# Two steps of the second compression placed later in the list of work

## The chip, the cores and the metric

The kernel runs on one core of a Trainium2 chip. The metric is the device time of one execution in microseconds, as the median of several runs. The engines are TensorE (PE in the profile, its weight loads PEld), VectorE (DVE), ScalarE (ACT), GpSimd (POOL) and SyncE (SP, which here only issues transfers).

## The reference, cut to what matters

One layer of a transformer on 512 tokens of width 1024: a mixer, a cross attention over 256 memory tokens and a gated feed-forward, each between norms. The mixer holds sparse attention beside an mLSTM. The change touches two parts of the mixer:

```python
def compress_blocks(kv, pos, w1, w2):            # once for k, once for v
    ...
    blocks = jnp.concatenate([c[:, :, :-1], c[:, :, 1:]], axis=3) + pos
    hid = jax.nn.silu(blocks.reshape(B, H, -1, CMP_BLOCK * DH) @ w1)   # (.., 2048) @ (2048, 256)
    return hid @ w2
...
    y_ml = jax.nn.sigmoid(mo) * hm               # mo: 512 columns of h @ w_in, the output gates
```

The compressed v is needed only by the compressed branch of the attention. `hm` is the mLSTM's output, of four heads.

## The kernel before

Every product of float32 matrices is made of three products in a shorter format: ScalarE writes a rounded copy of the weights (`hi`), VectorE or GpSimd subtracts it from the original (`lo`), and TensorE runs `lo*hi`, `hi*lo`, `hi*hi` (`split`, L166 and L167; `mm3`, L286 to L288). A tile of 128 output columns over 512 tokens (`dense_tiles`, L293 ff.) is thus one ScalarE copy and one subtraction of 128x1024 and 24 matmuls 512 columns wide into one PSUM bank.

After the first stage (norm of x, values, gates) comes a stage of mixed work, whose list is the string `order` in `PLAN`:

- `c0`, `c1`: projections of the mLSTM's q and k with their convolution (`ev_conv`, on VectorE); `kc`: projections that feed the two compressions (`ev_kcvc`); `m0`, `m2`: the four tiles of the output gates `mo`; `ks`: keys of the attention; `q0`: queries. Each has two tiles, and each mention of the name runs one of them. Their weights arrive in two buffers `raw`, filled by SP's queue; `hi` and `lo` (`whi`, `wlo`) take one each of **four** buffers `W`.
- `Sn`: the mLSTM's scores of head n (`mlstm_scores`): ScalarE and VectorE make `qm`, `kmA`, `kmB`; a row comes from DRAM into `rb` by a transfer that ScalarE's queue issues (L746); GpSimd adds a mask to it (`dg`, L748); ScalarE takes exponentials (L763); TensorE makes four blocks of scores, each in one of three PSUM banks `sc`; VectorE multiplies (L765). `On`: that head's output (`mlstm_out`: matmuls `bk_mn`, transposes `bk_mt`).
- `Lk`, `Lv`: loads of the compressions' weights; `Ck`, `Cv`: the compressions (`comp`), in four steps each. A step takes two of eight weight pieces (`w1s`). A piece is split in one buffer that holds `hi` and `lo` side by side, and is the moving side of two matmuls 512 wide into the bank `hb`, which is one of the three `sc` banks from the first step to the last. All eight pieces of `Cv` use the four `W` buffers (`"w1tv": "WWWWWWWW"`), and `"w1v": "pvpvvppv"` gives the engine of each subtraction: of pieces 0 to 7, numbers 0, 2, 5 and 6 on GpSimd and the rest on VectorE. Behind the eighth piece `comp_out` reads the bank.

The order on each engine is not the list's alone: a scheduler simulates the program at compile time and gives a free engine the first instruction in the list that its simulation holds ready. `S` and `O` are moved up in the list by 100 places (`mprio`). Buffers are handed out in the order so found. On the chip each engine then runs its queue in order.

The loop that reads the list is at the end of the stage's definitions:

```python
    for op in PLAN["order"].split():
        if op in whole:
            if op not in begun:
                begun[op] = whole[op]()
            run(begun[op], 1)
```

Of the kernel before, what the change touches and what calls it, by code (L numbers as in the profile page):

```python
# [47 lines left out]
def hybrid_layer(ctx, tc, a, out):  # L48
# [19 lines left out]


# [2 lines left out]

# [1 line left out]

# [1355 lines left out]
def build(inputs):  # L1430
    import numpy as np
    import concourse.bacc as bacc

    nc = bacc.Bacc("TRN2", target_bir_lowering=False, num_devices=1, dynamic_dma_scratch_size=1024)
    arrays, args = {}, {}
    for name in _INS + ["consts"]:
        v = np.ascontiguousarray(inputs[name] if name != "consts" else host_constants())
        arrays[f"in_{name}_dram"] = v
        args[name] = nc.dram_tensor(f"in_{name}_dram", v.shape, mybir.dt.from_np(v.dtype), kind="ExternalInput").ap()
    o = nc.dram_tensor("out_0_dram", (1, S, D), F32, kind="ExternalOutput").ap()  # L1440
    with tile.TileContext(nc, schedule_with_timeline_sim=True) as tc:
        hybrid_layer(tc, args, o)
    return nc, arrays
# [8 lines left out]
```

## Time and profile before

| | us |
|---|---|
| median of 3 runs | 838.19 |
| lowest, highest | 837.92, 840.44 |
| profiled execution, its own time | 842.27 |
| its span, as the profile shows it | 840.5 |

The span runs from the first to the last instruction of the profiled execution; 1.77 us of its own time lie around it. Times in the rows below are microseconds from the span's start. The stretch around the change lies between 100 and 145 us; the attention begins at some 165 us, and the rest follows to 840.5 us.

### The profile page before, as it was taken

The page shows a single profiled execution, that of the slowest core. Times are in us where ns is not written, and L with a number is a line of the kernel's source. Part 1 is how long each engine was busy: PE and PEld are TensorE (multiplying, and loading weights), DVE is VectorE, ACT ScalarE, POOL GpSimd, SP SyncE. Part 2 cuts the span into 40 slices and gives each one's busy share as a digit, 9 for nine tenths or more (in the row PEclk, how much of TensorE's full clock was granted, in tenths as well). Part 3 has the DMA queues.
Part 4 walks back from the last instruction along what each step waited for, and adds up shares of the span by engine and source line. Part 5 has one row for each costly group of instructions (what it writes and reads, how often), then busy time and mean ns, then how long its engine had stood idle before and what let it go on. Part 6 is the DMA issues. An engine that isn't in the chain of part 4 may idle for free.

```text
span 840.5 us, 12639 instructions
## 1 busy us (share of the span) xinstructions
PE 818.5 (97%) x4838; PEld 706.2 (84%) x4838; DVE 535.3 (64%) x936; ACT 424.8 (51%) x840; POOL 290.8 (35%) x218
## 2 busy tenths in 40 slices
PE   8999989989999999999999999999999999999997
PEld 6877858876689878778888899999999999888885
DVE  5766684897889735743553779877888885124323
ACT  5535566768768643633543465444444444334311
POOL 1015331455537343501420101444444444323320
PEclk9999989999999999999999999999999999999999
DMA  8238312221102431243323034333333323222102
GB/s 249 75 106 259 110 52 81 82 70 63 63 14 89 150 102 51 100 150 101 101 101 100 10 117 152 119 109 106 114 103 103 102 101 101 101 101 100 51 26 76
DMA packets 67763, 83.18 MB, mean 99 GB/s; under 512 B 4368, under 2 KB 53873, under 8 KB 67702
## 3 DMA queue, kind: packets, MB, share of 16 engines
q1 hardware_dynamic: 64574, 77.97, 28.8%
q10 hardware_dynamic: 3128, 4.40, 1.7%
q8 instruction: 38, 0.62, 0.3%
q14 instruction: 23, 0.19, 0.1%
HBM read 80.24 MB, written 2.12 MB: 98 GB/s over the span
## 4 chain that ended last, share of the span: by engine, by line
PE 88%; DVE 7%; ACT 2%; issue 2%; DMA 1%; POOL 0%; SPq 0%; DVEq 0%; ACTq 0%; POOLq 0%
PE bk_dT L286 6%; PE bk_dT L287 6%; PE bk_dT L288 6%; PE bk_X L1300 5%; PE bk_X L1301 5%; PE bk_X L1302 5%; PE bk_ff L287 5%; PE bk_ff L288 5%; PE bk_ff L286 5%; PE bk_pv L1026 3%; PE bk_dN L287 3%; PE bk_dN L286 3%; PE bk_dN L288 3%; PE bk_Z L1300 2%; PE bk_Z L1301 2%; PE bk_Z L1302 2%
## 5 line engine op out<-in xcount | busy, mean ns | idle before, releaser
L166 ACT ACTIVATE whi<-raw 128x1024 fp32r<-128x1024 f32 (+1 forms) x80 | 76.8, 967 | 72.0 <-PE bk_dT L286 35.3
L167 DVE TENSOR_TENSOR wlo<-raw,whi 128x1024 fp32r<-128x1024 f32 x43 | 56.7, 1322 | 85.9 <-PE bk_ff L287 43.0
L167 POOL TENSOR_TENSOR wlo<-raw,whi 128x1024 fp32r<-128x1024 f32 x21 | 50.3, 2396 | 121.4 <-ACT whi L166 119.5
L166 ACT ACTIVATE wh<-raw 128x1024 fp32r<-128x1024 f32 x64 | 67.2, 1057 | 49.3 <-PE bk_X L1300 17.7
L167 POOL TENSOR_TENSOR wl<-raw,wh 128x1024 fp32r<-128x1024 f32 x19 | 55.4, 2917 | 97.3 <-ACT wh L166 69.9
L286 PE MATMUL bk_dT<-hTh,wlo 128*128 128x512 f32 x192 | 77.6, 404 | 1.2 <-DVE wlo L167 0.9
L287 PE MATMUL bk_dT<-hTl,whi 128*128 128x512 f32 x192 | 76.9, 400 | 0.0
L288 PE MATMUL bk_dT<-hTh,whi 128*128 128x512 f32 x192 | 76.4, 398 | 0.0
L167 DVE TENSOR_TENSOR wl<-raw,wh 128x1024 fp32r<-128x1024 f32 x45 | 65.7, 1465 | 9.3 <-ACT wh L166 9.3
L1301 PE MATMUL bk_X<-A,wh 128*128 128x256 f32 x192 | 54.5, 284 | 1.0 <-DVE A L167 1.0
L167 POOL TENSOR_TENSOR gs<-gf,gs 128x512 fp32r<-128x512 f32 x22 | 32.4, 1477 | 65.9 <-ACT gs L166 65.9
L1300 PE MATMUL bk_X<-A,wl 128*128 128x256 f32 x192 | 54.4, 283 | 0.4 <-ACT A L166 0.4
L1302 PE MATMUL bk_X<-A,wh 128*128 128x256 f32 x192 | 54.3, 283 | 0.0
L287 PE MATMUL bk_ff<-wlo,gs 128*128 128x512 f32 x128 | 49.8, 389 | 0.0
L288 PE MATMUL bk_ff<-whi,gs 128*128 128x512 f32 x128 | 49.6, 389 | 0.0
L1300 PE MATMUL bk_X<-AS,wl 128*128 128x256 f32 x160 | 45.6, 285 | 2.4 <-ACT u L1355 2.3
L286 PE MATMUL bk_ff<-whi,gs 128*128 128x512 f32 x128 | 47.4, 389 | 0.0
L996 POOL TENSOR_SCALAR s<-s,acf 128x128 f32<-128x128 f32 (+3 forms) x32 | 36.3, 1146 | 26.7 <-PE bk_tr L1011 15.9
L286 PEld LDWEIGHTS bk_dT<-hTh,wlo 128*128 128x128 f32 x192 | 36.6, 191 | 10.4 <-DVE wlo L167 2.1
L1302 PE MATMUL bk_X<-AS,wh 128*128 128x256 f32 x160 | 44.9, 281 | 0.0
L1300 PE MATMUL bk_Z<-AS,wl 128*128 128x256 f32 x160 | 44.9, 280 | 0.0
L1301 PE MATMUL bk_X<-AS,wh 128*128 128x256 f32 x160 | 44.8, 280 | 0.0
(376 smaller groups left out, 2527.9 us busy)
## 6 DMA issues: line engine op xcount, KB each, us to landing
raw<-in_w_gate_up_dram SPq DMA_DIRECT2D x22, 1024.0 KB, 5.5
raw<-in_w_down_dram SPq DMA_DIRECT2D x11, 1024.0 KB, 4.9
raw<-in_w_xkv_dram SPq DMA_DIRECT2D x8, 1024.0 KB, 5.3
raw<-in_w_in_dram SPq DMA_DIRECT2D x7, 1024.0 KB, 5.2
raw<-in_w_out_dram SPq DMA_DIRECT2D x4, 1024.0 KB, 5.0
raw<-in_w_xq_dram SPq DMA_DIRECT2D x4, 1024.0 KB, 5.2
raw<-in_w_xo_dram SPq DMA_DIRECT2D x4, 1024.0 KB, 5.0
raw<-in_w_in_dram SPq DMA_DIRECT2D x6, 512.0 KB, 4.8
```

What stands on the lines that cost most here:

```text
L166: first = nc.scalar.activation(hi, src, AF.Copy)
L167: second = (eng or nc.vector).tensor_tensor(lo, src, hi.bitcast(F32), op=OP.subtract)
L286: nc.tensor.matmul(o, lhsT=wl, rhs=xh, start=start, stop=False)
L287: nc.tensor.matmul(o, lhsT=wh, rhs=xl, start=False, stop=False)
L288: return nc.tensor.matmul(o, lhsT=wh, rhs=xh, start=False, stop=stop).ins
L996: ENG[on].tensor_scalar(s[:, 0:n], s[:, 0:n], c, None, op0=OP.mult)
L1026: nc.tensor.matmul(o, lhsT=v, rhs=pTs[br][q][:, j], start=(br, j, q) == mms[0], stop=(br, j, q) == mms[-1])
L1300: nc.tensor.matmul(o, lhsT=wl[:, k, c], rhs=A.hi(n, k), start=st, stop=False, skip_group_check=True)
L1301: nc.tensor.matmul(o, lhsT=wh[:, k, c], rhs=A.lo(n, k), start=False, stop=False, skip_group_check=True)
L1302: nc.tensor.matmul(o, lhsT=wh[:, k, c], rhs=A.hi(n, k), start=False, stop=stop and k == 3, skip_group_check=True)
```

## The change

The list is rearranged in one place. The first and second step of `Cv` stay; the third comes behind the first tile of `m2`, and the fourth behind `S2`, ahead of the second tile of `m2`:

```diff
         "order": "c0 Lk c0 Lv kc m0 m0 Ck Ck Ck Ck c1 kc S0 O0 c1 "
-                 "S1 Cv Cv Cv Cv m2 S2 m2 O2 ks O1 ks q0 S3 q0 O3",
+                 "S1 Cv Cv m2 Cv S2 Cv m2 O2 ks O1 ks q0 S3 q0 O3",
```

No instruction, transfer or buffer is added or removed by name; their order, and what the scheduler makes of it, is all that differs.

## Rows read from the trace of the kernel before

**Rows 1.** The page, busy time of each engine and share of the span.

```profile
PE 818.5 (97%) x4838; PEld 706.2 (84%) x4838; DVE 535.3 (64%) x936; ACT 424.8 (51%) x840; POOL 290.8 (35%) x218
```

**Rows 2.** Busy time in stretches: bounds, length, each engine (instructions), granted clock, DMA, GB/s.

```profile
100.00:110.00 10.00, 10.00 (x54) 8.48 (x53) 9.52 (x24) 9.13 (x25) 3.27 (x4) 1.00 0.53 139
110.00:120.00 10.00, 7.56 (x29) 4.27 (x27) 9.62 (x20) 7.34 (x16) 5.48 (x4) 0.90 0.00 1
120.00:130.00 10.00, 9.22 (x34) 7.47 (x35) 5.23 (x11) 3.88 (x11) 2.64 (x3) 0.76 0.42 133
```

**Rows 3.** TensorE in order of time: start, length, line, tiles, [idle before, releaser].

```profile
110.80 1.18 PE L879 MATMUL bk_hb<-w1s,Xb 128*128 128x512 f32 x4
111.81 1.05 PE L776 MATMUL bk_mn<-mvx,sT 128*128 128x129 f32 x8
113.11 1.58 PE L879 MATMUL bk_hb<-w1s,Xb 128*128 128x512 f32 x4 [0.24 <-POOL w1s L167]
116.36 2.03 PE L879 MATMUL bk_hb<-w1s,Xb 128*128 128x512 f32 x6 [1.67 <-DVE w1s L167]
118.66 1.22 PE L879 MATMUL bk_hb<-w1s,Xb 128*128 128x512 f32 x2 [0.27 <-DVE w1s L167]
120.78 0.80 PE L286 MATMUL bk_dT<-hTh,wlo 128*128 128x512 f32 x1 [0.90 <-DVE wlo L167]
...
128.04 0.39 PE L288 MATMUL bk_dT<-hTh,whi 128*128 128x512 f32 x1
```

**Rows 4.** TensorE in one microsecond: bounds, length, busy, granted clock, DMA, GB/s.

```profile
118.00:119.00 1.00, 0.73 (x3) 0.50 0.00 0
```

**Rows 5.** The chain that ended last, pieces in order of time: start, length, what.

```profile
85.23 0.92 PE bk_hb L879 x4
...
122.85 0.43 PE bk_dT L287
```

**Rows 6.** ScalarE in order of time.

```profile
112.36 2.20 ACT L166 ACTIVATE w1s<-w 128x512 fp32r<-128x512 f32 x4
...
117.13 1.06 ACT L166 ACTIVATE whi<-raw 128x1024 fp32r<-128x1024 f32 x1 [1.77 <-PE bk_hb L879]
...
122.50 0.33 ACTq L746 DMA_DIRECT2D rb<-rd  x1
...
142.41 1.06 ACT L166 ACTIVATE whi<-raw 128x1024 fp32r<-128x1024 f32 x1 [2.87 <-PE bk_dT L286]
```

**Rows 7.** VectorE in order of time.

```profile
113.23 0.68 DVE L167 TENSOR_TENSOR w1s<-w,w1s 128x512 fp32r<-128x512 f32 x1
...
113.89 0.74 DVE L712 SCALAR_TENSOR_TENSOR zc<-u,chan,zc 128x509 f32<-128x509 f32 x1
114.55 1.75 DVE L167 TENSOR_TENSOR w1s<-w,w1s 128x512 fp32r<-128x512 f32 x1
...
119.51 2.35 DVE L167 TENSOR_TENSOR wlo<-raw,whi 128x1024 fp32r<-128x1024 f32 x2
```

**Rows 8.** GpSimd in order of time.

```profile
114.10 3.35 POOL L167 TENSOR_TENSOR w1s<-w,w1s 128x512 fp32r<-128x512 f32 x2 [1.05 <-ACT w1s L166]
...
128.33 1.28 POOL L748 TENSOR_TENSOR dg<-rb,cc 128x512 f32<-128x512 f32 x1 [4.62 <-DMA rb<-rd]
```

**Rows 9.** Splits of the tile `w1s` from 100 to 120; ns min/median/max, first and last start.

```profile
L166 ACT ACTIVATE w1s<-w x8: 613/620/631, 103.1 to 114.7; 128x512 fp32r<-128x512 f32 x8
L167 POOL TENSOR_TENSOR w1s<-w,w1s x4: 1385/1633/1737, 103.8 to 115.7; 128x512 fp32r<-128x512 f32 x4
L167 DVE TENSOR_TENSOR w1s<-w,w1s x4: 679/689/1755, 106.8 to 117.9; 128x512 fp32r<-128x512 f32 x4
```

**Rows 10.** The same view for `wlo` on VectorE from 40 to 260.

```profile
L167 DVE TENSOR_TENSOR wlo<-raw,whi x9: 1211/1224/1599, 39.8 to 168.5; 128x1024 fp32r<-128x1024 f32 x9
```

**Rows 11.** Issues of SP's queue in order of time.

```profile
121.88 16.45 SPq L300 DMA_DIRECT2D raw<-in_w_in_dram  x2
...
171.15 1.29 SPq L442 DMA_DIRECT2D nB<-fd  x3
```

## The prediction

> **What bounds the kernel now.** I read the page first: TensorE is busy for 97% of the span and no other engine for more than 64% (VectorE) [rows 1]. So the end moves by what TensorE loses or wins back, and a change in the order of work can win only where TensorE stands still or runs slowly. The second view was the table of stretches. It shows such a place in the middle of the second compression: TensorE is fully busy from 100 to 110, busy for 7.56 of 10 us in the next stretch, and from 120 to 130 it is busy again but at a granted clock of 0.76 on average [rows 2]. The engine that is full there is VectorE, with 9.52 and 9.62 of 10 us [rows 2].
>
> The third view, TensorE in order of time, tells what happens. The 16 matmuls of `Cv` begin at 110.80 and the last pair starts at 118.66 and after; between them TensorE waits for a subtraction on GpSimd, for one on VectorE (1.67 us) and for a second one (0.27 us), and then 0.90 us more for the `wlo` of the first tile of `m2` [rows 3]. A busy time in these rows covers pipelined matmuls; the starts are what count. While TensorE worked this thinly its clock fell: at 118 to 119 it is at 0.50 [rows 4], that is the lower of its two levels, 1.2 instead of 2.4 GHz, and a 512 wide matmul takes 0.43 us where four take 0.92 us, 0.23 each, at the upper level [rows 5]. Nine of the 24 matmuls of the first `m2` tile run so, 9 x (0.43 - 0.23) = 1.8 us.
>
> How much is there to win? From 110.80 the work is 16 matmuls of `Cv` at 0.23 (3.7 us), the eight `bk_mn` (1.0 us) and 24 of `m2` at 0.23 (5.5 us): 10.2 us, which would end at 121.0. The 24th starts at 128.04 [rows 3] and ends at 128.27. So 7.3 us are lost here, 0.9% of the time, and that is the ceiling of the gain.
>
> **Why TensorE waits.** The eight pieces share the four buffers `W`. ScalarE copies pieces 3 to 6 in a row from 112.36 as the matmuls of earlier pieces free a buffer, then the first `whi` of `m2` has to wait for the matmuls on `hb` (1.77 us idle) and starts at 117.13 [rows 6]. VectorE has the subtraction of piece 3 until 113.91, steps of c1's convolution (`zc`), piece 4 for 1.75 us, and only at 119.51 the two `wlo` [rows 7]; GpSimd subtracts pieces 5 and 6 from 114.10 to 117.45 [rows 8]. TensorE has 24 matmuls of `m2` to do that depend on nothing of this, whose weights are there, but whose buffers and VectorE's time come behind all of `Cv`.
>
> **The change, step by step.** It adds and removes no instruction. It puts the `hi` and `lo` of the first `m2` tile ahead of pieces 4 to 7. The steps, each from the rows of before:
>
> 1. Up to piece 3 all stays. ScalarE has copied piece 3 by 112.36 + 2.20/4 = 112.9. The buffers of pieces 0 and 1, which went to pieces 4 and 5, now go to `whi` and `wlo`. `whi` takes 1.06 us [rows 6]: 114.0.
> 2. VectorE is done with piece 3 at 113.91; I leave the `zc` step of 0.74 us in front, to 114.6 [rows 7]. `wlo` takes 1.22 us (median) [rows 10]: 115.8. TensorE has by then finished pieces 2 and 3, at about 114.5, and waits 1.3 us.
> 3. The 24 matmuls run from 115.8 for 5.5 us at the upper level, to 121.3. They cover the splits of pieces 4 and 5, for which two buffers are left: 0.62 us on ScalarE each, then at most 1.76 us on VectorE and 1.74 us on GpSimd [rows 9]. If this cover were gone they would cost what they cost now.
> 4. Pieces 4 and 5, four matmuls, 0.92 us: 122.2.
> 5. Pieces 6 and 7 get the buffers that `m2` leaves at 121.3: 0.62 us on ScalarE, 1.39 us for piece 6 on GpSimd [rows 9], ready at 123.3. TensorE waits 1.1 us, then 0.92 us: 124.2. This is the new wait that the change brings; ahead of it on TensorE the scores of `S2` may fill it, which I don't count.
> 6. The second `m2` tile, which before was split together with the first (2.35 us for both `wlo` [rows 7]) and ready at once, takes the buffers of pieces 4 and 5. ScalarE is done with piece 7 at 122.5; `whi` 1.06 and `wlo` 1.22 us: 124.8. TensorE waits 0.6 us.
>
> The second tile thus starts at 124.8 instead of 128.27, a gain of 3.5 us. Of the 7.3 us, 3.8 thus stay: the three waits of steps 2, 5 and 6 (3.0 us) and what pieces 2 and 3 lose up to 114.5 now as before (0.8 us).
>
> **The queues and what comes after.** Neither moved step issues a transfer on SP's queue: `Lv` stays. SP's next read of weights, at 121.88, waits until the second `m2` tile is split, at 121.86 before and 124.8 now; its first user on ScalarE stands at 142.41 [rows 6, 11], so 2.9 us later costs nothing. The last step issues one small transfer on ScalarE's queue (`w2`), whose result is wanted behind `comp_out`. What `comp_out` makes, the compressed v, is wanted only where the attention's units end, so a later end of `Cv` costs nothing by itself; but `hb` keeps one of three `sc` banks while `S2` wants four in turn. From `S2` on nothing is bound to the clock on the wall: even the last loads of the bias tables, issued at 171.15 [rows 11], wait for buffers that TensorE's own `bk_mn` frees. So the 3.5 us should last to the end.
>
> By the profiled execution: 842.27 - 3.5 = 838.8 us. That execution is 4.1 us above the median of the runs, so for the median I take 838.19 - 3.5 = **834.7 us**. The bounds of this case: with every wait gone, 838.19 - 7.3 = 830.9; with the waits of steps 2, 5 and 6 longer by a third (1.0 us in all), 835.7. 0.3% is 2.5 us, about what a measurement of this kernel can tell from no change.
>
> **Rival 1: GpSimd's queue, slower.** `S2` stands now ahead of the last step of `Cv`. Its `dg` waits on GpSimd for the row `rb` from DRAM: the transfer was issued at 122.50 [rows 6] and `dg` ran only at 128.33, after 4.62 us of standing still [rows 8]. If the scheduler's simulation holds `dg` ready before piece 6, the subtraction of piece 6 is queued behind it and starts at 128.33 + 1.28 = 129.6; it is ready at 131.0, the four matmuls end at 131.9, and the second `m2` tile starts 3.6 us later than before and, behind such a gap, at the lower clock (1.8 us): 838.19 + 5.4 = 843.6. It decides from the point where piece 6 is ready later than 128.1. For it: `S2` is ahead in the list and moved up by 100 places. Against it: before, GpSimd got `dg` 11 us after its last piece [rows 8], and piece 6 needs to come only by 123.3. Chance 0.20.
>
> **Rival 2: VectorE slowed beside GpSimd, no change.** The same subtraction of `w1s` takes 0.69 us on VectorE in the median and 1.755 us where GpSimd's pieces 5 and 6 run beside it [rows 7, 8, 9]. If piece 5 on GpSimd falls on the `wlo` of step 2, that takes 1.22 x 1.755/0.689 = 3.1 us, 1.9 us more, and the gain is 1.6 us: 836.6. If the clock falls too in the longer gap, nothing is left: 838.4. I put the change nearer to 1.22 because piece 5 has to wait for a buffer that piece 3 frees at 114.5 and for a copy of 0.62 us, so that most of `wlo` is past by then; the largest of nine `wlo` is 1.599 us [rows 10]. The Trainium skill, page "GPSIMD Engine Reference", section "Key points", says that GpSimd shares its interfaces to SBUF with VectorE and that they contend when VectorE reads two inputs from SBUF, as this subtraction does; the trace agrees, with 1.755 against 0.689 us, and by that rule taken for the whole of `wlo` the time would be 836.6. Chance 0.14.
>
> **Rival 3: the change doesn't do what it says.** The list is not the queue. `S` and `O` move, and the simulation may hand the buffers to pieces 4 to 7 first anyway, as their copies need only ScalarE. Then TensorE's order stays nearly as it is: 838.2. Against it: before, the engines' order around `Cv` and `m2` is the list's. Chance 0.14.
>
> **How the numbers follow.** The forecast has 0.52, the rivals 0.20, 0.14 and 0.14. Faster is the forecast alone, 0.52; within 0.3% are rivals 2 and 3, 0.28; slower is rival 1, 0.20. The predicted time is the forecast's. Its own range is 830.9 to 835.7. For eight in ten the range has to take in the cases without change up to the 2.5 us that count as such, so 830.9 to 840.7; the slower rival stays outside.
>
> **What would show it.** Right: on TensorE four `bk_hb` pairs, then `bk_dT` without a break at some 115 to 121, then `bk_hb` again; `wlo` on VectorE near 114.6 instead of 119.51; a clock that doesn't fall, or for fewer than the nine `m2` matmuls of before; the start of the second `m2` tile near 124.8. The forecast is wrong if a piece of `Cv` stands on GpSimd behind `dg` or another instruction that waits (rival 1), if `wlo` takes around 3 us (rival 2), if `whi` still stands behind piece 7 on ScalarE (rival 3), or if a wait that did not exist opens behind 145 us, which would mean that the order further down was rearranged too.

## The result and the profile after

| | us | runs |
|---|---|---|
| kernel before, median (lowest to highest) | 838.92 (837.92 to 840.44) | 4 |
| changed kernel, median (lowest to highest) | 844.70 (843.31 to 846.22) | 4 |
| ratio, 95% interval | 1.0072 [1.0055, 1.0088] | |
| predicted | 834.7 (830.9 to 840.7), faster | |

The change made the kernel slower by 0.7%. The prediction is 10 us off and on the wrong side. The profiled execution of the changed kernel took 844.43 us of its own time, with a span of 842.6 us.

The table of stretches comes first, with the same columns as [rows 2]; the last two stretches lie far behind the change.

```profile
110.00:120.00 10.00, 8.49 (x39) 6.26 (x38) 9.18 (x20) 5.69 (x14) 3.60 (x3) 1.00 0.00 1
120.00:130.00 10.00, 7.77 (x31) 5.68 (x30) 9.05 (x15) 8.62 (x19) 6.33 (x8) 0.90 0.21 59
...
128.00:129.00 1.00, 1.00 (x4) 0.77 (x3) 1.00 (x3) 1.00 (x2) 0.12 (x1) 0.50 0.44 42
...
150.00:160.00 10.00, 9.13 (x48) 7.23 (x47) 6.74 (x14) 8.81 (x23) 4.64 (x3) 1.00 0.26 73
180.00:200.00 20.00, 15.18 (x75) 11.04 (x73) 17.59 (x58) 13.47 (x39) 14.05 (x11) 0.91 0.17 54
```

From 100 to 110 TensorE is busy throughout, as before. From 110 to 120 TensorE is busier than before, 8.49 against 7.56 us, at full clock; from 120 to 130 it is less busy, 7.77 against 9.22 [rows 2]. The gain is there and is given back within ten microseconds, with a stretch at the lower level of the clock behind it (0.50 at 128 to 129; before it was at 118 [rows 4]). From 150 to 160 TensorE was busy throughout in the trace of before and is now for 9.13 us.

TensorE in order of time shows the local part; these rows answer to [rows 3].

```profile
113.15 1.59 PE L879 MATMUL bk_hb<-w1s,Xb 128*128 128x512 f32 x4 [0.24 <-POOL w1s L167]
115.87 0.50 PE L286 MATMUL bk_dT<-hTh,wlo 128*128 128x512 f32 x1 [1.13 <-DVE wlo L167]
...
121.53 1.10 PE L879 MATMUL bk_hb<-w1s,Xb 128*128 128x512 f32 x4
123.75 0.74 PE L879 MATMUL bk_hb<-w1s,Xb 128*128 128x512 f32 x2
125.72 0.73 PE L879 MATMUL bk_hb<-w1s,Xb 128*128 128x512 f32 x2 [1.23 <-DVE w1s L167]
127.45 0.49 PE L286 MATMUL bk_dT<-hTh,wlo 128*128 128x512 f32 x1 [1.00 <-DVE wlo L167]
```

The first `m2` tile, pieces 4 and 5, piece 6, piece 7 and the second `m2` tile follow each other. The other three engines, in the same view:

```profile
114.60 1.22 DVE L167 TENSOR_TENSOR wlo<-raw,whi 128x1024 fp32r<-128x1024 f32 x1
...
122.84 1.14 DVE L723 TENSOR_SCALAR sg<-sg,chan 128x512 f32<-128x512 f32 x1 [0.33 <-ACT sg L722]
123.90 1.76 DVE L167 TENSOR_TENSOR w1s<-w,w1s 128x512 fp32r<-128x512 f32 x1
125.59 0.68 DVE L795 TENSOR_TENSOR ym<-bk_mt,sg 128x512 f32<-128x512 f32 x1
126.19 1.21 DVE L167 TENSOR_TENSOR wlo<-raw,whi 128x1024 fp32r<-128x1024 f32 x1
...
123.57 0.99 ACT L763 ACTIVATE sT<-rb,ub 128x128 f32<-128x128 f32 x3 [0.23 <-DMA rb<-rd]
124.46 1.04 ACT L166 ACTIVATE whi<-raw 128x1024 fp32r<-128x1024 f32 x1
...
122.41 1.29 POOL L167 TENSOR_TENSOR w1s<-w,w1s 128x512 fp32r<-128x512 f32 x1 [0.81 <-ACT w1s L166]
123.66 1.46 POOL L748 TENSOR_TENSOR dg<-rb,cc 128x512 f32<-128x512 f32 x1
125.17 2.20 POOL L733 MEMSET kB<- 64x512 f32 x4
```

Piece 6 on GpSimd comes ahead of `dg`. Piece 7 on VectorE takes 1.76 us, with `dg` beside it on GpSimd, in place of 0.69 [rows 9]. On ScalarE the `whi` of the second tile stands behind the first exponentials of `S2`.

The next place is 25 us further down. GpSimd, VectorE, TensorE:

```profile
152.46 1.29 POOL L748 TENSOR_TENSOR dg<-rb,cc 128x512 f32<-128x512 f32 x1 [24.33 <-DMA rb<-rd]
153.71 1.03 POOL L236 TENSOR_TENSOR rs_r<-rs_e,mhalf 128x4 f32<-128x4 f32 x1
154.70 2.39 POOL L167 TENSOR_TENSOR wlo<-raw,whi 128x1024 fp32r<-128x1024 f32 x1
...
154.77 3.00 DVE L790 TENSOR_SCALAR hnat<-hnat,rs_r 128x128 f32<-128x128 f32 x4 [2.17 <-POOL rs_r L236]
...
157.32 0.30 PE L791 MATMUL bk_mt<-cc,hnat 128*128 128x128 f32 x1 [0.28 <-DVE hnat L790]
159.48 0.47 PE L286 MATMUL bk_dT<-hTh,wlo 128*128 128x512 f32 x1 [0.59 <-DVE kB L841]
```

In the trace of before, TensorE has no wait of 0.1 us or more from 136 to 165. Here `rs_r`, the factor that scales head 2's output, comes behind `S3`'s `dg`. The four scalings of `hnat` then begin together with GpSimd's residual split of `q0`'s second tile and take 3.00 us, where those of an earlier head take 0.86 us at 121.66. And at the attention's start, VectorE and TensorE:

```profile
179.01 1.14 DVE L447 COPY nB<-nB 128x256 f32<-128x256 f32 x1 [0.63 <-DMA nB<-fd]
180.07 0.41 DVE L683 TENSOR_TENSOR pc<-pc,bk_pc 128x256 f32<-128x256 f32 x1
...
183.14 1.09 DVE L687 TENSOR_TENSOR pc<-pc,mn 128x512 f32<-128x512 f32 x1
...
187.31 0.63 PE L697 MATMUL bk_pcT<-cc,pc 128*128 128x128 f32 x4 [1.68 <-ACT qst L827]
189.52 0.69 PE L791 MATMUL bk_mt<-cc,hnat 128*128 128x128 f32 x2 [1.36 <-DVE hnat L790]
```

The last bias tables are loaded from 175.62 on, 4.5 us later than before [rows 11]. VectorE's copy of one of them (head 6's) now stands in the middle of the chain on `pc`, the compressed branch's probabilities, ahead of the second `bk_pc` addition. In the trace of before it is done by 177.0, ahead of the chain's first addition at 177.39:

```profile
176.54 0.43 DVE L447 COPY nB<-nB 128x256 f32<-128x256 f32 x1
```

From its first addition to its last product (L694) the chain takes 10.8 us here and 9.2 us in the trace of before. The row of `bk_pcT` names ScalarE's `qst`, which ended just before; but in both traces the transposes start 0.15 us behind the end of the last product on `pc`, so it is the chain that they wait for.

**Where the time is lost.** To compare executions at equal work, I went through TensorE's instructions and took from the time that had passed what each kind takes when it runs without a gap at the upper level (0.23 us for 512 columns; from the kernel before). What is left was lost to waits and to the lower clock. The segments have the same amount of work in every kernel; in the trace of before they end at some 111, 140, 165 and 230 us.

| us lost by TensorE | up to `Cv` | `Cv`, `m2` | to the attention | its first units | rest | span |
|---|---|---|---|---|---|---|
| before (the profile of the prediction) | 11.3 | 8.3 | 1.2 | 11.4 | 30.8 | 840.5 |
| before, a second profile (e1) | 10.0 | 6.4 | 1.2 | 11.7 | 31.1 | 837.9 |
| after | 11.3 | 7.7 | 2.6 | 13.1 | 30.4 | 842.6 |

Nothing that the change moves stands ahead of `Cv`, so the first column differs by chance (8.5 to 11.4 us over all profiles here). The clock differs by chance too: before and e1 have the same instructions in the same order, and their 1.9 us in the second column are nearly all of it clock. Against e1, the changed kernel is 4.7 us longer: 1.3 of it ahead of the change, 1.3 in `Cv` and `m2`, 2.8 in the two segments behind, less 0.7 in the rest.

### The profile page after: what moved, and what is told of

Its sections match the earlier page's. It is cut to its first block, busy times and chain, and to the rows that moved or that the text cites. A ratio compares the mean times of both kernels' runs of the same rounds, so it can differ in the third digit from the quotient of the medians.

```text
span 842.6 us, 12635 instructions
## 1 busy us (share of the span) xinstructions
PE 816.8 (97%) x4838; PEld 705.0 (84%) x4838; DVE 533.7 (63%) x936; ACT 424.5 (50%) x840; POOL 290.9 (35%) x218
## 4 chain that ended last, share of the span: by engine, by line
PE 71%; DVE 6%; ACT 2%; issue 1%; POOL 0%; DMA 0%; DVEq 0%; ACTq 0%; POOLq 0%
PE bk_X L1300 5%; PE bk_X L1301 5%; PE bk_X L1302 5%; PE bk_ff L286 5%; PE bk_ff L288 5%; PE bk_ff L287 5%; PE bk_pv L1026 3%; PE bk_dT L286 3%; PE bk_dT L287 3%; PE bk_dT L288 3%; PE bk_dN L287 3%; PE bk_dN L286 3%; PE bk_dN L288 3%; PE bk_Z L1300 2%; PE bk_Z L1301 2%; PE bk_Z L1302 2%
## 5 line engine op out<-in xcount | busy, mean ns | idle before, releaser
L167 POOL TENSOR_TENSOR wlo<-raw,whi 128x1024 fp32r<-128x1024 f32 x21 | 50.5, 2405 | 119.2 <-ACT whi L166 109.7
```

The costliest lines, as they stand in the source:

```text
L167: second = (eng or nc.vector).tensor_tensor(lo, src, hi.bitcast(F32), op=OP.subtract)
```

## The experiments

The theories went in with letters. A: the loss comes from the order further down. B: it comes from new waits beside the change. C: the profile that I started from was an unlucky one. Later D stands for the two places further down, L for the local part and P for the chain on `pc`. Each time is a median of 4 to 12 runs; each ratio is to runs of the kernel before on the same chip, and four chips were used.

| run | median, us | ratio to before, 95% interval |
|---|---|---|
| e1 before, unchanged | 839.10 | 0.9995 [0.9981, 1.0009] |
| e2 `Cv` together, `S2` behind `m2` | 840.05 | 1.0007 [0.9991, 1.0023] |
| e3 step 4 alone moved | 842.40 | 1.0046 [1.0029, 1.0063] |
| e4 after, `dg` behind `rs_r` | 844.77 | 1.0058 [1.0036, 1.0080] |
| e5 after, head 6's copy on ScalarE | 843.23 | 1.0043 [1.0027, 1.0060] |
| e6 after, `q0`'s second split on VectorE | 841.24 | 1.0022 [1.0009, 1.0035] |
| e7 after, both | 839.19 | 0.9996 [0.9984, 1.0009] |
| e8 step 4 behind the second `m2` tile | 843.80 | 1.0048 [1.0030, 1.0065] |
| e9 before, both edits | 840.59 | 1.0021 [1.0000, 1.0042] |
| e10 e8, both edits | 840.78 | 1.0022 [1.0007, 1.0036] |
| e11 e8, head 6's copy on ScalarE, one split at 227 us moved | 842.09 | 1.0033 [1.0014, 1.0051] |
| e12 e7, head 2's `dg` on VectorE | 843.48 | 1.0052 [1.0035, 1.0069] |
| e13 e10, `pc` chain one unit later | 847.42 | 1.0100 [1.0080, 1.0121] |
| e14 e10, `pc` chain two units later | 847.72 | 1.0104 [1.0083, 1.0124] |
| e15 before, `pc` chain one unit later | 842.23 | 1.0042 [1.0025, 1.0059] |

### Before again, and the parts of the order (e1 to e4)

e1 has no edit. 

> The kernel before, unchanged. Theory C (the profiled execution of before was an unlucky one, 842.27 against a median of 838.9, because TensorE's clock stood at half for 6.8 us at 118 and again at 186; the usual execution has less of that, so that part of the 7.3 us I wanted to win back is usually not lost): ratio 1.000, and this profile's span is 836 to 838, with half-clock stretches that are together at least 5 us shorter. If C is wrong the span is 840 to 841 again with two stretches of 6.8 us, and the difference to the median lies elsewhere.

Its profile lost 6.4 us in `Cv` and `m2` where the profile of the prediction lost 8.3. The difference is the clock: in e1 TensorE's granted clock is 0.83 on average from 110 to 120 and 1.00 from 120 to 130, where [rows 2] has 0.90 and 0.76. So the stretch from which I read the ceiling of 7.3 us was about 2 us worse than in this execution of the same kernel. Theory C held for the span (837.9 us), but not in size: the time at the lower clock is 3.4 us shorter, not 5.

```diff
-  "S1 Cv Cv m2 Cv S2 Cv m2 O2 ..."   # after
+  "S1 Cv Cv Cv Cv m2 m2 S2 O2 ..."   # e2
+  "S1 Cv Cv Cv m2 S2 Cv m2 O2 ..."   # e3
```

e2: 

> The four steps of Cv stay together as before; only S2 is listed behind the second tile of m2. The queues stay as before up to the second m2 tile and differ behind it. Theory A (what costs the time is the order that the scheduler makes further down, from 140 to 230, which any rearrangement shuffles): a ratio that is off 1 by more than 0.2% in either direction, with the local stretch from 108 to 135 as before. Theory B (the local stretch itself, by the new waits): ratio 0.998 to 1.002, since the local stretch is untouched.

e3: 

> Only the fourth step of Cv comes behind the first tile of m2. Theory B: the new waits are those of the last two pieces and of the second m2 tile, and they are here too, with a first part as before (pieces 4 and 5 in a row): 842 to 845, TensorE loses as much from 108 to 135 as in the changed kernel or more. Theory A: the local stretch loses 1 to 3 us less than before, and the sum is decided by 140 to 230.

e2 is the time of before, which goes against theory A as it stood: not every rearrangement costs time. e3, with half of the change, costs 0.46%, and none of it in `Cv` and `m2` (6.5 us lost, as in e1): 3.2 us are lost up to the attention (1.2 in e1) and 13.8 in its first units (11.7). So an order can cost time far behind the place at which it differs.

e4 holds `S3`'s `dg` on GpSimd until head 2's `rs_r` is through:

```diff
-        nc.gpsimd.tensor_tensor(dg, ...)
+        with (tc.issue_after(pow_of[2]) if h == 3 else ExitStack()):
+            nc.gpsimd.tensor_tensor(dg, ...)
```

> The changed kernel with one edge of order on GpSimd: S3's mask addition dg is queued behind the norm factor of head 2 instead of ahead of it (24.3 us of standing still before dg in the changed kernel). Theory A: the factor comes 1.2 us earlier, VectorE's four scalings no longer run beside GpSimd's next subtraction (3.0 us there, 0.9 alone), and TensorE loses 1.0 to 1.5 us less between 150 and 162: 842.5 to 844. Theory B: no change to the changed kernel, 844 to 845.

No gain, against theory A's 842.5 to 844: `rs_r` came 0.94 us earlier, at 152.77, but the scalings got slower. VectorE and GpSimd in e4:

```profile
153.83 4.01 DVE L790 TENSOR_SCALAR hnat<-hnat,rs_r 128x128 f32<-128x128 f32 x4 [1.21 <-POOL rs_r L236]
...
155.01 2.37 POOL L167 TENSOR_TENSOR wlo<-raw,whi 128x1024 fp32r<-128x1024 f32 x1
```

The order of `dg` and `rs_r` is not what delays `hnat`. What GpSimd runs beside VectorE is: first `dg`, at 153.77, then the split.

### The two places further down (e5 to e7, control e9)

```diff
-        "bias": "vaappavp",
+        "bias": "vaappaap",     # e5, e7, e9 to e14: head 6's copy on ScalarE
-        "q0": "vp",
+        "q0": "vv",             # e6, e7, e9, e10, e12 to e14: second split of q0 on VectorE
```

e5: 

> The changed kernel (844.7 us) with one copy moved: head 6's half of the bias table nB goes from VectorE to ScalarE. All else but some thirty places in the queues near 180 us stays. Theory D (the order further down): in the changed kernel this copy stands inside the pc chain at 179.01 us, takes 1.14 us and waits 0.63 us for its load; without it the chain ends up to 1.6 us earlier: 843.1 to 843.9 us. Rival R (the attention's start is set by something else, such as its transfers, and the copy is covered): 844.4 to 845 us.

e6: 

> The changed kernel with the residual split of the second tile of q0 taken from GpSimd to VectorE. Theory D: in the changed kernel that split runs on GpSimd from 154.70 us for 2.39 us, just while VectorE scales hnat four times, which take 3.00 us in place of 0.87; TensorE loses some 1.4 us in waits for hnat and kB. With the split on VectorE (1.2 us, ahead of the scalings) the four scalings take 0.9 us, the transposes start by 155.6 and the total is 843.3 us, 842.8 to 844.0. Rival R (VectorE only takes on what GpSimd lost; what follows has slack): 844.4 to 845.5 us.

e7: 

> Both edits, head 6's copy on ScalarE and the second residual split of q0 on VectorE, in the changed kernel. Theory D: the two places are apart in time and their gains add: 842.0 us (841.2 to 843.0), which is the 844.7 less 1.4 and less 1.3. Rival R: 844.4 to 845.5 us.

e6 came out 1.5 us slower than before (841.24 against 839.71 on the same chip) in place of 5.8, and e7 level with before; both are faster than theory D had forecast, by 2.1 and 2.8 us. In e6 the scalings take 0.88 us again (156.15 us) and no wait for `hnat` or `kB` is left from 136 to 165. e5 has 1.5 us less than the changed kernel by the medians, but its interval overlaps with that of the change, and in its trace the pc chain is no shorter: TensorE waits 1.68 us ahead of `bk_pcT` in both, since the chain's subtraction (L687) now takes 1.87 us, in place of 1.09, beside a split on GpSimd.

How this comes about is seen best in e6 and e7: the order on every engine is the same in both but for that one copy. e6, VectorE, GpSimd and TensorE in order of time:

```profile
179.24 0.98 DVE L447 COPY nB<-nB 128x256 f32<-128x256 f32 x1 [1.04 <-DMA nB<-fd]
180.14 2.89 DVE L687 TENSOR_TENSOR pc<-pc,mn 128x512 f32<-128x512 f32 x1
...
179.98 2.50 POOL L167 TENSOR_TENSOR wlo<-raw,whi 128x1024 fp32r<-128x1024 f32 x1
...
185.19 0.44 PE L976 MATMUL bk_sc<-kA,qst 128*128 128x384 f32 x1 [1.72 <-DVE mx L980]
```

e7, the same view:

```profile
176.51 1.23 DVE L687 TENSOR_TENSOR pc<-pc,mn 128x512 f32<-128x512 f32 x1
...
179.54 1.75 DVE L234 TENSOR_SCALAR rs_e<-mss 128x4 f32<-128x4 f32 x1
...
178.86 2.41 POOL L167 TENSOR_TENSOR wlo<-raw,whi 128x1024 fp32r<-128x1024 f32 x1
...
181.70 0.43 PE L976 MATMUL bk_sc<-kA,qst 128*128 128x384 f32 x1
```

In e6 the copy waits 1.04 us for its load, and VectorE with it. The subtraction behind it then falls on GpSimd's split and is done at 183.03, half a microsecond after the split's end. Without the copy the subtraction is through before that split begins. TensorE's wait ahead of `bk_pcT` is the same in both (1.56 and 1.57 us); what is gone in e7 is the wait for `mx` (the row minima of a block of scores), which VectorE makes behind the subtraction: the matmul that waits 1.72 us for it in e6, at 185.19, starts at 181.70 without a wait. At equal instructions e6 is 1.6 us behind e7 ahead of this place, 3.5 us at this matmul, and 4.0 from 193 on, as its clock falls too (0.83 from 180 to 200, and 1.00 in e7). The medians differ by 2.0 us, with twelve runs each; the intervals of the two ratios meet at 1.0009.

e9 is the kernel before with both edits. 

> The kernel before with the same two edits as in the run of both (head 6's copy of nB on ScalarE, the second residual split of q0 on VectorE). Theory D (the two waits stand in the order that the change brings about, and are not there before): within 1 us of the kernel before, 838.5 to 840.5. Rival (the two edits save some 5 us in any order, and the changed order still costs as much as before): 834 to 836.5 us.

It is not faster than before, and a tenth of a us above theory D's range. The two edits save nothing in the old order; in the new one they give back, by the medians, all that the change had cost. The edit of e6 changes TensorE's order from 157 us on too (29.1 us lost in the rest, 30.4 in the changed kernel), so a part of its gain may come from there; e6 and e7 differ by the copy alone. Of the 5.5 us between the medians of the changed kernel and e7, the two traces show 2.8 us from `Cv` on: some 1.1 us less up to the attention, 2.1 less in its first units and 1.2 less in the rest, but 1.6 more in `Cv` and `m2`, where e7's clock was lower (0.83 from 110 to 120, 1.00 in the changed kernel). The other half is ahead of `Cv`, where e7's execution lost 8.5 us and that of the changed kernel 11.3, and can't be put down to the edits. So the medians show that the loss lies in the order behind the change; how much of it is each of the two places, the traces leave open.

### The local gain (e8, e12)

e8 puts step 4 behind the second tile of `m2`:

```diff
-                 "S1 Cv Cv m2 Cv S2 Cv m2 O2 ks O1 ks q0 S3 q0 O3",
+                 "S1 Cv Cv m2 Cv m2 Cv S2 O2 ks O1 ks q0 S3 q0 O3",
```

> The order of the changed kernel with step 4 behind the second output-gate tile (S1 Cv Cv m2 Cv m2 Cv S2), so that the split of the second tile is neither behind the third nor behind the fourth step's piece on ScalarE and VectorE. Theory L (the 3.5 us of the forecast were made and given back because the second tile's split stood behind piece 7 and S2's exponentials): the second tile starts by 125 us in place of 127.45 and TensorE loses 3 us less up to there; if nothing else moved, 842 us, but the order further down is arranged anew. Rival (the second tile waits for its load or for other work): it starts at 127 us or later.

TensorE and ScalarE in e8:

```profile
122.20 1.10 PE L879 MATMUL bk_hb<-w1s,Xb 128*128 128x512 f32 x4
124.72 0.50 PE L286 MATMUL bk_dT<-hTh,wlo 128*128 128x512 f32 x1 [0.16 <-DVE wlo L167]
...
188.94 1.09 PE L697 MATMUL bk_pcT<-cc,pc 128*128 128x128 f32 x4 [4.07 <-DVE pc L694]
...
122.35 1.06 ACT L166 ACTIVATE whi<-raw 128x1024 fp32r<-128x1024 f32 x1
124.28 0.99 ACT L763 ACTIVATE sT<-rb,ub 128x128 f32<-128x128 f32 x3 [0.38 <-DMA rb<-rd]
```

`whi` stands ahead of `S2`'s exponentials, the second tile starts at 124.72 (I had forecast 124.8), the clock stays at 1.00, and 4.8 us are lost in `Cv` and `m2` in place of 8.3: the forecast's 3.5 us, of which 1.6 remain against the 6.4 of e1. The total doesn't have them: TensorE waits 4.07 us for `pc` at 188.94.

e12 is e7 with one tensor_tensor of head 2 moved:

```diff
-        nc.gpsimd.tensor_tensor(dg, ...)
+        (nc.vector if h == 2 else nc.gpsimd).tensor_tensor(dg, ...)
```

> The changed kernel with both edits (839.2 us), and head 2's dg (one tensor_tensor of 128x512) on VectorE in place of GpSimd, so that piece 7's residual split on VectorE has no two-input instruction of GpSimd beside it. Theory L (VectorE's instructions stand still until GpSimd's ends): that split takes 0.70 us in place of 1.77, the wait ahead of the last two bk_hb goes from 0.94 to under 0.3 us, and the second output-gate tile starts 0.5 to 1 us earlier relative to piece 4; total 838.4 (837 to 841, as the planner moves other work). Rival (it is the memory that is shared with loads, or ScalarE's part that is late): the split still takes over 1.3 us.

TensorE, VectorE and ScalarE in e12:

```profile
118.71 1.10 PE L879 MATMUL bk_hb<-w1s,Xb 128*128 128x512 f32 x4
122.52 0.72 PE L879 MATMUL bk_hb<-w1s,Xb 128*128 128x512 f32 x2 [0.86 <-DVE w1s L167]
124.25 0.79 PE L286 MATMUL bk_dT<-hTh,wlo 128*128 128x512 f32 x1 [1.01 <-DVE wlo L167]
...
121.78 0.68 DVE L167 TENSOR_TENSOR w1s<-w,w1s 128x512 fp32r<-128x512 f32 x1
...
121.67 1.04 ACT L166 ACTIVATE whi<-raw 128x1024 fp32r<-128x1024 f32 x1
```

Half of the expectation held. With GpSimd free of `dg`, piece 7 takes 0.68 us, so it was `dg` that slowed it. But the wait ahead of the last two `bk_hb` is 0.86 us, not under 0.3, and the second tile comes no earlier: it starts 5.54 us behind the matmuls of piece 4 here, 5.51 us in e7 and 5.92 in the changed kernel. `whi` still ends only 4.0 us behind them, at 122.71, and VectorE, which now does `dg` itself, comes to `wlo` at 122.98. So a shorter queue on VectorE alone can win little here; that the order on ScalarE is the rest of the delay was not tried by itself (e8 takes away both). The total, 843.48 in place of 838.4, says nothing of the local part, since TensorE's order is another from 133 us on.

### Where a real local gain goes (e10, e11, e13 to e15)

e10 is e8's order with both edits. 

> The order with step 4 behind the second output-gate tile (it measured 843.8), with the two edits. In its profile the local gain of 3.4 us was there and the pc chain of the attention's start lost it (TensorE waited 4.07 us for pc at 188.94 us). Theory D (what follows decides, and the two edits take away GpSimd's split beside VectorE and a copy of 0.44 us in the pc chain): 840 to 842 us, and lower the more of the 4.07 us goes. Rival (the pc chain there is late for other reasons): 843 to 845 us.

e11 has e8's order, head 6's copy on ScalarE, and the edit below. 

> The same order (step 4 last), with head 6's copy on ScalarE and the first residual split of Y on VectorE in place of GpSimd: in that order's profile GpSimd's residual splits (wlo and two of yml, 174.13 to 178.96 us) stood ahead of the memset of pc and beside VectorE's scalings of s (L996), of which two took 2.97 us. If GpSimd's splits make the pc chain late: 839.5 to 842 us, with the memset of pc 1 to 2 us earlier. If not: 843 to 845 us.

```diff
-        "ysplit": "pvvp",
+        "ysplit": "vvvp",
```

Both lose 4.2 us in `Cv` and `m2`, 2.2 less than e1, and neither is faster than before; e10 lies in theory D's range. In the attention's first units they lose 14.4 and 16.1 us, where the two profiles of before lose 11.4 and 11.7. TensorE waits 3.16 us for `pc` in e10 and 4.39 us in e11.

e11 did not test what it was meant to. GpSimd in e11:

```profile
172.29 2.35 POOL L167 TENSOR_TENSOR wlo<-raw,whi 128x1024 fp32r<-128x1024 f32 x1 [3.49 <-ACT whi L166]
174.60 2.52 POOL L167 TENSOR_TENSOR yml<-ym,ymh 128x512 fp32r<-128x512 f32 x2
177.06 0.53 POOL L670 MEMSET pc<- 128x512 f32 x1
```

The three splits that I suspected still stand ahead of the memset of `pc`. `ysplit` gives the engines for another tensor, whose split (`yTl`) ran on GpSimd at 227 us in e8; up to there GpSimd's order in e11 is that of e8. e10 says more on the guess: there the memset runs at 170.81, ahead of those splits and 2.8 us before the chain's first addition, and TensorE still waits 3.16 us.

To see whether the pc chain is what holds the gain, I moved it in the list of fillers, first for e10, then for before:

```diff
-        "fill": ["C", "", "", "q", ...
+        "fill": ["", "C", "", "q", ...   # e13, e15 (before)
+        "fill": ["", "", "C", "q", ...   # e14
```

e13: 

> The run with step 4 last and both edits (840.8), with the compressed branch of the first key head (the pc chain) one attention unit later in the list. In that run the local gain of some 4 us was still there at the start of the attention and TensorE then waited 3.16 us for pc (184.94 us). Theory P (the pc chain on VectorE is what the gain runs into; TensorE has other units to do meanwhile): that wait falls below 1 us and the total is 837.5 to 839 us. Rival (VectorE has the same work to do in any order, and another wait of the same length takes its place): 840 to 842 us.

e14: 

> The same with the pc chain two units later. Theory P: 836.5 to 839 us, no wait for pc. Rival: 840 to 842 us.

e15: 

> Control: the kernel before with the pc chain one unit later. If moving it is a gain of its own and has nothing to do with this change, the kernel before gains as much as the run above (2 to 3 us: 836 to 837). Theory P: before's wait for pc is 0.85 us, with 1.3 us ahead of it, so at most 1 us: 838 to 839.5 us.

Theory P falls, and the times of e13 and e14 are far above its rival's 840 to 842 us as well. TensorE in e13:

```profile
185.25 0.66 PE L1011 MATMUL bk_tr<-cc,s 128*128 128x128 f32 x2 [2.73 <-ACT pT L1018]
187.32 0.69 PE L976 MATMUL bk_sc<-kA,qst 128*128 128x384 f32 x1 [0.77 <-DVE mx L980]
...
197.34 1.09 PE L697 MATMUL bk_pcT<-cc,pc 128*128 128x128 f32 x4 [1.66 <-DVE pc L694]
```

The wait for `pc` is shorter, and waits for ScalarE's `pT` and VectorE's `mx` stand in its place; the first units lose 19.3 and 20.4 us. The kernel before loses time by the move too (14.2 us there). So the place of the pc chain is not the cause by itself. What is shown: in e8, e10 and e11 the attention's first units swallow what TensorE gains ahead of them. Added up from the start of `Cv` to their end, e1 lost 19.3 us, e8 22.6, e10 20.1 and e11 22.1, though the last three were 1.6 to 2.2 us ahead of e1 behind `m2`. In part it is the clock: from 180 to 200 it is 0.74 on average in e8 and e11, 0.61 in e13 and 0.55 in e14, where e1 has 0.83. But e10 has 0.83 too, and its 2.7 us more than e1 there are waits. Why there are more of them in e8's order, beyond the single ones named, stays open; no version here beats the kernel before.

## Why the prediction was wrong

**Steps 1 to 4 were right.** `wlo` on VectorE came at 114.60 with 1.22 us, the first tile started at 115.87 after a wait of 1.13 us (forecast 115.8 and 1.3), pieces 4 and 5 followed at 121.53, and the clock stayed at 1.00 from 110 to 120.

**Steps 5 and 6 were wrong in size.** Piece 6 was ready at 123.70, near the 123.3 of step 5. But step 5 priced only piece 6. Piece 7, on VectorE, came behind `sg` (the output gates; 1.14 us, beside piece 6 on GpSimd; 0.48 in e12) and took 1.76 us beside `dg`, so that the last pair of matmuls started at 125.72 where I had the whole step end at 124.2. In step 6 I let `whi` follow piece 7 at once on ScalarE, at 122.5; piece 7's copy ended at 123.33, three exponentials of `S2` stood between, and `whi` ran from 124.46 to 125.50. Its subtraction came later still, at 126.19, since VectorE had piece 7 and `ym` (a head's output times its gates) ahead of it. The second tile started at 127.45, not 124.8; 1.3 us of that is work of `S2` and of another head, which TensorE did from 122.47 on while it waited. Behind two waits of 1.23 and 1.00 us it ran at 0.50 from 128 on. Of the 3.5 us 0.6 were left against the profile of the prediction (7.7 lost, 8.3 before). e8, with 3.5 us, shows that the arithmetic was sound where those two are not in the way.

**"So the 3.5 us should last to the end" was wrong in kind.** This is the step that cost most. I argued that nothing behind `S2` is bound to the clock on the wall and so took the rest as a shift. It is not shifted: the engines' orders there are arranged anew, and they put a split on GpSimd beside the scalings of `hnat`, and a copy into the pc chain. The changed kernel lost 2.8 us more than e1 between `m2` and the end of the attention's first units, and 1.3 us in `Cv` and `m2`. By the medians of e6, e7 and e9, moving that split and that copy to other engines gives back the whole loss in the new order and nothing in the old one; the move of the split also rearranges what follows, and the traces of the changed kernel and of e7 show about half of the 5.5 us from `Cv` on. I had named such a rearrangement only as a thing that would show me wrong (a wait behind 145 us); it had no chance of its own. And e8 and e10 show that a gain that did last to the attention is lost there.

**The base.** I took a gain worked out in one execution, 4.1 us above the median, off the median. e1 shows that about 2 us of the stretch's loss were that execution's clock.

**The rivals.** Rival 1 did not happen: piece 6 was subtracted at 122.41, ahead of `dg`; that the measured time is near its 843.6 us is luck. Rival 2's mechanism did, though not on the `wlo` of step 2, where GpSimd was idle until 115.48: it took piece 7, `hnat` and the pc chain. Rival 3 did not.

## What to carry to other kernels

Where a planner sets the order of each engine, a moved step is a new order for everything behind it: give "the order further down changes" its own chance and price, from the waits that the later stages are just short of. A local gain can end at the next stage that another engine paces, as those of e8, e10 and e11 did at the attention's first units; look there first, and compare at equal work against more than one profile of the kernel before. When pricing an instruction on VectorE, look for what GpSimd runs beside it (piece 7: 1.76 us, and 0.68 with `dg` gone), and move one of the two before moving the work on TensorE. And look in the trace for the instruction that an edit was to move, before reading its time: e11 moved another one.

## What the runs showed of the hardware

A VectorE instruction that begins while GpSimd's elementwise instruction on two inputs runs can stand until that one ends, however small it is. In e7 `rs_e`, of four columns, took 1.75 us in place of 0.16 (at 185.59 in the changed kernel) and ended at 181.29; GpSimd's split ended at 181.27. In the changed kernel, the scalings of `hnat` one by one:

```profile
L790 DVE TENSOR_SCALAR hnat<-hnat,rs_r x4: 273/278/2405, 154.8 to 157.5; 128x128 f32<-128x128 f32 x4
```

One of the four takes 2405 ns and the others 273 to 278 (shortest, median, longest): GpSimd's split ran until 157.09. So here it is not a share of each instruction's speed. A memset on GpSimd did no such thing: `wlo` at 126.19 took 1.21 us beside one of 2.20 us. GpSimd can be held up in turn: in e6 its `rs_r` of four columns took 2.01 us in place of 1.03, beside a `wlo` on VectorE of 1.54 us that had begun earlier. The Trainium skill, page "GPSIMD Engine Reference", section "Key points", names two kinds of VectorE instructions that contend, those with two inputs from SBUF and those in a mode that uses two ports. The traces agree for the first (piece 7, with 1.76 against 0.68 us); that `rs_e` and the scalings, of one input, are of the second kind is not something that a run here shows.

The same instructions ahead of `Cv` lost between 8.5 and 11.4 us from one profiled execution to the next, which is more than the local effect of the change.
